# A two-layer encoder in fp32r matmuls: input-norm rows spread by matmuls with ones, output projection with its contraction outside, and adding transfers for one weight set a layer

## The chip, the cores and the metric

The kernel runs on one core of one Trainium2 chip. The metric is the device time of one execution in microseconds (us), as a median over several runs. All times below are us unless marked ns. The engines are PE (TensorE; PEld is its weight load), DVE (VectorE), ACT (ScalarE), POOL (GpSimd) and SP (SyncE, which here only issues transfers).

## The reference

512 tokens of width 1024 pass an input LayerNorm and two layers. A layer has three token mixers, a gated merge of their outputs, an output projection and a SwiGLU feed-forward network (FFN), with a LayerNorm behind each residual sum:

```python
x = layer_norm(x, ln_in_g, ln_in_b)
for l in range(2):
    proj = x @ w_in[l]
    na, df, ml = neighbourhood(...), differential(...), latent(...)
    merged = sum(sigmoid(gate[b]) * (branch[b] @ w_branch[l, b]) for b in range(3))
    x = layer_norm(alpha * x + merged @ w_out[l], ln1_g[l], ln1_b[l])
    g, u = split(x @ w_ffn_in[l])              # 1024 -> 2 x 2816
    x = layer_norm(alpha * x + (silu(g) * u) @ w_ffn_out[l], ln2_g[l], ln2_b[l])
```

## The kernel before

Tokens are held as four tiles of 128 rows (`xt[t]`, width 1024) and, transposed and split, as `xth` and `xtl`. Every fp32 matmul is made of three fp32r products of a high and a low part (`mm3`, L155 to L158). Weights come in chunks of 512 KB by SP's queue into `raw` (two buffers); `wsplit` (L134) makes the high part on ACT (`whi`, L138) and the low part on DVE (`wlo`, L139), as a rule at high priority. A DVE or ACT operation of width 512 that is not a weight's split is mostly L221 and L222, the two halves of `split`.

Two families of slots hold the rest: `R` (38 of width 512) and `H` (8 of width 1024, named f0 to f7), both first in, first out. PSUM has four tags with two banks each: `acc`, `sc`, `pv` and `tr`. A scheduler sets the order on each engine when the program is built; code under `tc.high_priority()` is placed ahead of other work that is ready.

The places that matter here:

- **The start** (L280 to L294). SP loads the first token tile, the constants, the LayerNorm's scale and shift (`load_gb`, L266 to L271: one 4 KB row each, broadcast by the transfer to 128 partitions, 512 KB each), the second tile and two weight chunks. For each tile `layer_norm` (L234) takes statistics (L237, L239), a power on POOL, then the two passes L252 and L253 on DVE; for columns from `SPREAD` on, the passes go to ACT and POOL instead (L247 to L249). `to_xt` (L258) transposes a tile on PE in two groups of four (L263) and splits them (L221, L222).
- **The output projection** (`out_proj`, L701). For each half of 512 output columns it loads four weight chunks, and then, token tile by token tile, runs all eight contraction steps into one `acc` bank and adds the bank to the residual (L711). Between the halves `ahead()` takes the loads of the plain FFN weights (`plain_weights`; issued at L206, split by L221 and L222). The second half yields each tile to the LayerNorm and the transposes.
- **The FFN.** The first set of 256 hidden columns is `ffn_plain`. The ten other sets of a layer run as `ffn_fast` (L813): seven products of quarter size (L778) in place of eight, on sums of weight quarters (L839 s = u0 + u1, L840 u0 = g0 - u0, L841 g0 = s - g0, L853 g1 = g1 - g0, each 1024 wide on DVE) and on sums of `x` quarters, made once a layer by `x_sums` (L732, the adds at L748 to L759). The first fast set of a layer, `early`, loads its weights while the LayerNorm before it still runs; its first product is copied out by ACT (L833, `p1`), and the results are added at L844, L848 and later lines.

Of the kernel before, what the change touches and what calls it, by code (L numbers as in the profile page):

```python
# [20 lines left out]
D_FF = 2816  # L21
# [60 lines left out]
def trunk(ctx, tc, x, ln_in, w_in, feat, bias, lamv, w_mla, w_mlr, w_mlv, w_branch, w_out,  # L82
# [28 lines left out]
    ring = cp.tile([128, 256], F32, name="ring")  # L111
    at = [0]

# [166 lines left out]
    G.memset(expo, -0.5)  # L280
    load_x(0)
    nc.sync.dma_start(cons, cst)
    gb = load_gb(ln_in)
    na_v, na_slots = [], []
# [416 lines left out]
    def out_proj(xt, mg, l, ahead):  # L701
        act = tuple(KTiles(m) for m in mg)
        for hf in range(2):
            if hf == 1:
                ahead()
            c = slice(hf * 512, (hf + 1) * 512)
            ch = wload_ks(lambda a, e: [w_out[l, a:e, c]], 512, (2, 2, 2, 2))
            for t in range(NT):
                p = bank("acc")
                gemm_x(p, ch, slice(0, 512), act, tsl(t), KD)  # L710
                V.scalar_tensor_tensor(xt[t][:, c], xt[t][:, c], ALPHA, p, op0=OP.mult, op1=OP.add)  # L711
                if hf == 1:
                    yield t
        R.put(*mg[0], *mg[1])
# [17 lines left out]
    def x_sums():  # L732
# [5 lines left out]
        for i in range(2):  # L738
            ts = gate_tiles() + [dp.tile([128, 512], F32, tag="o32", name="xs", bufs=1)]
            t1, t2, d = (two(t) for t in ts)  # L740
            q = lambda a: a[:, 2 * i:2 * i + 2]

            def halves(n, t):
                hl = (R.get(), R.get())
                split(*hl, t)
                res[n].append(hl)

            V.tensor_sub(t1, q(h(0, 1)), q(h(0, 0)))  # L748
            V.tensor_sub(d, q(lo(0, 1)), q(lo(0, 0)))
            V.tensor_add(t1, t1, d)  # L750
            V.tensor_sub(t2, q(h(1, 1)), t1)
            V.tensor_add(t2, t2, q(lo(1, 1)))
            halves(1, ts[1])
            halves(0, ts[0])
            V.tensor_sub(d, t2, q(h(0, 0)))
            V.tensor_sub(d, d, q(lo(0, 0)))
            halves(2, ts[2])
            V.tensor_sub(t1, q(h(1, 0)), t2)
            V.tensor_add(t1, t1, q(lo(1, 0)))  # L759
            halves(3, ts[0])  # L760
# [19 lines left out]

    def hidden(gate, up):

        sg = ptile()
        A.activation(sg, gate, AF.Silu)
        V.tensor_mul(sg, sg, up)
        hl = (R.get(), R.get())
# [26 lines left out]
    def ffn_fast(l, m, sums):  # L813
# [3 lines left out]

        def load(t, base, kh):
            c = slice(base + m * 128, base + (m + 2) * 128)
            nc.sync.dma_start(t.rearrange("p (k c) -> p k c", k=4),  # L820
                              w_ffn_in[l, kh * 512:(kh + 1) * 512, c].rearrange("(k p) c -> p k c", p=128))
            return t
# [3 lines left out]

        g0, u0, u1 = load(H.get(), 0, 0), load(H.get(), D_FF, 0), load(H.get(), D_FF, 1)
        s = H.get()
        g1 = load(wp.tile([128, 1024], F32, tag="raw", name="raw", bufs=2), 0, 1)
        px, py, pz = bank("sc"), bank("pv"), bank("sc")  # L830
# [7 lines left out]
        with tc.high_priority():  # L838
            V.tensor_add(s, u0, u1)  # L839
            V.tensor_sub(u0, g0, u0)  # L840
            V.tensor_sub(g0, s, g0)  # L841
        product(py, halved(g0), from_sum(t2), True)
# [9 lines left out]
        with tc.high_priority():  # L852
            V.tensor_sub(g1, g1, g0)  # L853
        product(pz, halved(g1), from_x(1, 1), False)
        V.tensor_add(u2, pz, u2)
        product(py, halved(u1), from_sum(t4), False)
        V.tensor_add(p1, py, p1)
        H.put(s, u0, g0, u1)
        res = [hidden(px, p1)]
        res.append(hidden(u2, u3))  # L860
        return res
# [228 lines left out]
```

## Time and profile before

| what | value |
|---|---|
| median of 3 runs | 1858.38 us (1858.06 to 1862.17) |
| profiled execution | 1861.61 us, span 1859.6 us |
| PE busy | 1814.6 us, 98% of the span |
| DVE, ACT, POOL busy | 1331.0 (72%), 905.3 (49%), 88.2 (5%) us |
| transfers | 34.5% of 16 engines over the span, 105 GB/s |
| granted TensorE clock, mean | 0.996 |

A share of busy time is a mean over stages. The profiled execution is 3.2 us above the median of the runs shown; 2.0 of its 1861.61 us lie outside the span. A row of a timeline gives start, duration and, in brackets, how long the engine stood idle before and which work ended that wait. A row's duration is longer than its share of a queue when instructions overlap: what an instruction adds to its engine's queue is the distance to the next start.

### The profile page before, as it was taken

How to read it: one execution, taken by the hardware profiler on the slowest of the kernel's cores; microseconds unless marked ns; L12 is line 12 of the kernel's file. 1: busy time of each engine (PE TensorE's matmuls, PEld its weight loads, DVE VectorE, ACT ScalarE, POOL GpSimd, SP SyncE). 2: the span in 40 equal slices, each digit the busy share in tenths (PEclk: the TensorE clock that was granted, in tenths of full speed). 3: DMA queues.
4: the chain of work that ended last, by engine and by line, in shares of the span. 5: the costliest groups of instructions: out<-in, count | busy, mean ns of one | idle time of the engine just before them, and what ended most of it. 6: DMA issues, size and time to landing. Idle time of an engine off the chain costs nothing.

```text
span 1859.6 us, 28547 instructions
## 1 busy us (share of the span) xinstructions
PE 1814.6 (98%) x11200; PEld 1617.4 (87%) x11200; DVE 1331.0 (72%) x2228; ACT 905.3 (49%) x1620; POOL 88.2 (5%) x165
## 2 busy tenths in 40 slices
PE   6999999999999899999999999999999999999997
PEld 5988899988878899999789888999888789999996
DVE  6478887665568977777756888866655698677766
ACT  3467776555433433434326677755554244343431
POOL 4100000000001000000001000000000000000001
PEclk9999999999999999999999999999999999999999
DMA  7453332223251233333445432322233512333332
GB/s 250 119 166 88 88 101 74 79 81 85 90 193 58 69 104 101 102 103 102 148 124 156 124 97 87 90 65 86 74 97 109 174 57 90 105 95 110 92 101 79
DMA packets 167765, 195.86 MB, mean 105 GB/s; under 512 B 8528, under 2 KB 132688, under 8 KB 167632
## 3 DMA queue, kind: packets, MB, share of 16 engines
q1 hardware_dynamic: 167632, 194.05, 34.5%
q8 instruction: 88, 1.44, 0.3%
q14 instruction: 45, 0.37, 0.1%
HBM read 177.24 MB, written 9.44 MB: 100 GB/s over the span
## 4 chain that ended last, share of the span: by engine, by line
PE 89%; DVE 4%; DMA 3%; ACT 2%; issue 1%; POOL 1%; POOLq 0%; SPq 0%; DVEq 0%; ACTq 0%
PE acc L156 18%; PE acc L157 18%; PE acc L158 18%; PE sc L778 11%; PE pv L778 8%; PE tr L648 2%; DVE wlo L139 1%; PE pv L491 1%; DMA raw<-in_w_ffn_in_dram 1%; ACT whi L138 1%; PE pv L656 1%; PE pv L655 1%; PE sc L477 1%; PE sc L632 1%; PE sc L631 1%
## 5 line engine op out<-in xcount | busy, mean ns | idle before, releaser
L139 DVE TENSOR_TENSOR wlo<-raw,whi 128x1024 fp32r<-128x1024 f32 (+4 forms) x242 | 288.0, 1191 | 137.0 <-ACT whi L138 132.2
L138 ACT ACTIVATE whi<-raw 128x1024 fp32r<-128x1024 f32 (+4 forms) x242 | 250.0, 1034 | 267.4 <-DMA raw<-in_w_ffn_out_dram 50.9
L138 ACT ACTIVATE whi<-f 128x1024 fp32r<-128x1024 f32 x100 | 104.9, 1057 | 222.4 <-PE acc L158 127.3
L156 PE MATMUL acc<-xth,whi 128*128 128x512 f32 x512 | 203.9, 398 | 0.1
L158 PE MATMUL acc<-xth,wlo 128*128 128x512 f32 x512 | 202.8, 396 | 0.0
L157 PE MATMUL acc<-xtl,whi 128*128 128x512 f32 x512 | 202.6, 396 | 0.0
L156 PE MATMUL acc<-whi,r 128*128 128x512 f32 (+1 forms) x504 | 194.7, 392 | 4.6 <-DVE f L711 3.9
L157 PE MATMUL acc<-wlo,r 128*128 128x512 f32 (+1 forms) x504 | 197.3, 391 | 1.1 <-DVE wlo L139 1.1
L158 PE MATMUL acc<-whi,r 128*128 128x512 f32 (+1 forms) x504 | 197.0, 391 | 0.0
L778 PE MATMUL pv<-r,whi 128*128 128x256 f32 x960 | 175.8, 282 | 9.9 <-DVE P L844 4.8
L156 PE MATMUL acc<-whi,xth 128*128 128x256 f32 (+2 forms) x544 | 161.6, 299 | 2.1 <-ACT whi L138 2.1
L157 PE MATMUL acc<-wlo,xth 128*128 128x256 f32 (+2 forms) x544 | 162.1, 299 | 1.3 <-DVE wlo L139 1.3
L158 PE MATMUL acc<-whi,xtl 128*128 128x256 f32 (+2 forms) x544 | 162.1, 299 | 0.0
L778 PEld LDWEIGHTS pv<-r,whi 128*128 128x128 f32 x960 | 148.2, 189 | 13.4 <-DVE P L844 5.2
L139 DVE TENSOR_TENSOR wlo<-f,whi 128x1024 fp32r<-128x1024 f32 x100 | 121.6, 1221 | 26.0 <-ACT whi L138 25.8
L778 PE MATMUL pv<-r,wlo 128*128 128x256 f32 x480 | 134.7, 281 | 0.0
L778 PE MATMUL sc<-xth,whi 128*128 128x256 f32 x480 | 133.9, 280 | 0.7 <-ACT P L833 0.7
L778 PE MATMUL sc<-xtl,whi 128*128 128x256 f32 x480 | 133.7, 279 | 0.0
L778 PE MATMUL sc<-xth,wlo 128*128 128x256 f32 x480 | 133.3, 279 | 0.0
L156 PEld LDWEIGHTS acc<-whi,r 128*128 128x128 f32 x504 | 94.3, 188 | 26.9 <-DVE f L711 4.7
L157 PEld LDWEIGHTS acc<-wlo,r 128*128 128x128 f32 x504 | 95.0, 188 | 22.1 <-DVE wlo L139 1.8
L158 PEld LDWEIGHTS acc<-whi,r 128*128 128x128 f32 x504 | 94.9, 188 | 21.0
(235 smaller groups left out, 4285.3 us busy)
## 6 DMA issues: line engine op xcount, KB each, us to landing
raw<-in_w_in_dram SPq DMA_DIRECT2D x64, 512.0 KB, 3.8
f<-in_w_ffn_in_dram SPq DMA_DIRECT2D x60, 512.0 KB, 3.7
raw<-in_w_ffn_out_dram SPq DMA_DIRECT2D x44, 512.0 KB, 3.8
raw<-in_w_in_dram SPq DMA_DIRECT2D x64, 256.0 KB, 3.3
raw<-in_w_ffn_in_dram SPq DMA_DIRECT2D x28, 512.0 KB, 3.6
raw<-in_w_branch_dram SPq DMA_DIRECT2D x24, 512.0 KB, 3.5
raw<-in_w_out_dram SPq DMA_DIRECT2D x16, 512.0 KB, 3.8
r<-r SPq DMA_DIRECT2D x56, 128.0 KB, 2.9
```

The source lines that it names most:

```text
L138: A.activation(hi[:, :n], raw[:, :n], AF.Copy)
L139: V.tensor_sub(lo[:, :n], raw[:, :n], f32(hi[:, :n]))
L156: T.matmul(o, lh[0], rh[0], start=first, stop=False)
L157: T.matmul(o, lh[0], rh[1], start=False, stop=False)
L158: T.matmul(o, lh[1], rh[0], start=False, stop=last)
L477: T.matmul(sc, qs[j][:, tsl(t)], ks[j][1], start=False, stop=True)
L491: T.matmul(po[:, 0:256], ch_[:, tsl(k)], v, start=k == 0, stop=False)
L631: T.matmul(sc, q[0][:, tsl(t)], k[0], start=True, stop=False)
L632: T.matmul(sc, q[0][:, tsl(t)], k[1], start=False, stop=False)
L648: T.transpose(pt[:, tsl(i)], prs[i % 2][:, tsl(kp + i // 2)], ident)
L655: T.matmul(oc, v, ph[:, c], start=kt == 0, stop=False)
L778: T.matmul(o[:, c], w[a][:, j, f], x[e], start=fresh and mi == 0 and j == 0 and n == 0, stop=j == 3 and n == 2, skip_group_check=True)
```

## The change

1. **Start.** The first token tile comes in two halves, from SP's and ACT's queue. The LayerNorm's scale and shift come as two rows of 4 KB into one partition each; four matmuls with a row of ones (contraction 1) spread them over the partitions into `sc` and `pv` banks, and four ACT copies bring them to SBUF.
2. **Output projection.** In the first half the loop over weight chunks is outside and the four token tiles inside, each with a bank of its own (sc, sc, pv, pv), all added to the residual at the end. The second half keeps its loops, but its chunks are now asked for behind the plain FFN weights' place: `ahead()` has moved behind `wload_ks`.
3. **Early set.** For the first fast set of each layer, s is loaded as u0 and then u1 is added to it by a transfer that accumulates, issued by POOL; g0 is added to u0 in the same way. The two DVE adds of these fall away in this set. So that sums are enough, signs are flipped in the `x` sums, the weight sums and in `hidden` (by a form of instruction with a factor), for all sets. The slots are taken and returned in another order.

```diff
-    load_x(0)
+    nc.sync.dma_start(xt[0][:, 0:512], x[0:128, 0:512])
+    nc.scalar.dma_start(xt[0][:, 512:1024], x[0:128, 512:1024])
     nc.sync.dma_start(cons, cst)
-    gb = load_gb(ln_in)
+    rows = [H.get() for _ in range(2)]
+    for i in range(2):
+        nc.sync.dma_start(rows[i][0:1], ln_in[i:i + 1, :])
+    ones = ring[0:1, 0:128]
+    V.memset(ones, 1.0)
+    gb = []
+    for i, tag in enumerate(("sc", "pv")):
+        t = H.get()
+        for hf in range(2):
+            c = slice(hf * 512, (hf + 1) * 512)
+            p = bank(tag)
+            T.matmul(p, ones, rows[i][0:1, c], start=True, stop=True)
+            A.activation(t[:, c], p, AF.Copy)
+        gb.append(t)
+    H.put(*rows)
...
         for hf in range(2):
-            if hf == 1:
-                ahead()
             c = slice(hf * 512, (hf + 1) * 512)
             ch = wload_ks(lambda a, e: [w_out[l, a:e, c]], 512, (2, 2, 2, 2))
+            if hf == 0:
+                ps4 = [bank(i) for i in ("sc", "sc", "pv", "pv")]
+                for part in ch:
+                    for t in range(NT):
+                        gemm_x(ps4[t], [part], slice(0, 512), act, tsl(t), KD)
+                for t in range(NT):
+                    V.scalar_tensor_tensor(xt[t][:, c], xt[t][:, c], ALPHA, ps4[t], op0=OP.mult, op1=OP.add)
+                continue
+            ahead()
             for t in range(NT):
...
-            V.tensor_sub(t2, q(h(1, 1)), t1)
-            V.tensor_add(t2, t2, q(lo(1, 1)))
+            less(t2, q(h(1, 1)), t1)
+            V.tensor_sub(t2, t2, q(lo(1, 1)))
...
-        V.tensor_mul(sg, sg, up)
+        V.scalar_tensor_tensor(sg, up, sign, sg, op0=OP.mult, op1=OP.mult)
...
+            if add:
+                nc.gpsimd.dma_start(dst, src, accum_op=OP.add)
+            else:
+                nc.sync.dma_start(dst, src)
...
-        g0, u0, u1 = load(H.get(), 0, 0), load(H.get(), D_FF, 0), load(H.get(), D_FF, 1)
+        g0 = load(H.get(), 0, 0)
         s = H.get()
+        u0, u1 = load(H.get(), D_FF, 0), load(H.get(), D_FF, 1)
+        if early:
+            load(load(s, D_FF, 0), D_FF, 1, True)
+            load(u0, 0, 0, True)
...
         with tc.high_priority():
-            V.tensor_add(s, u0, u1)
-            V.tensor_sub(u0, g0, u0)
-            V.tensor_sub(g0, s, g0)
+            if not early:
+                V.tensor_add(s, u0, u1)
+                V.tensor_add(u0, g0, u0)
+            V.tensor_add(g0, s, g0)
...
         with tc.high_priority():
-            V.tensor_sub(g1, g1, g0)
+            V.tensor_add(g1, g1, g0)
...
-        H.put(s, u0, g0, u1)
+        H.put(g0, s, u0, u1)
```

Three places show what this does to the order of the engines. The rows name line, operation, output, inputs and shape.

DVE at the start, before (f0 and f1 are the first two token tiles, f4 and f5 the scale and the shift, tr a bank of transposes, wlo a low part of a weight chunk):

```order
L237 BN_STATS ring_126<-f0_112 128x6 x2
L239 BN_AGGR ring_126<-ring_126 128x2
L252 SCALAR_TENSOR_TENSOR f0_112<-f0_112,ring_126,f4_116 128x512
L252 SCALAR_TENSOR_TENSOR f0_112<-f0_112,ring_126,f4_116 128x256
L253 SCALAR_TENSOR_TENSOR f0_112<-f0_112,ring_126,f5_117 128x512
L253 SCALAR_TENSOR_TENSOR f0_112<-f0_112,ring_126,f5_117 128x256
L237 BN_STATS ring_126<-f1_113 128x6 x2
L222 TENSOR_TENSOR xtl_73<-tr_161,xth_72 128x4x128
```

The same place now (f6 and f7 are the scale and the shift):

```order
L252 SCALAR_TENSOR_TENSOR f0_112<-f0_112,ring_126,f6_118 128x512
L239 BN_AGGR ring_126<-ring_126 128x2
L252 SCALAR_TENSOR_TENSOR f1_113<-f1_113,ring_126,f6_118 128x512
L139 TENSOR_TENSOR wlo_150<-raw_147,whi_149 128x1024
L252 SCALAR_TENSOR_TENSOR f0_112<-f0_112,ring_126,f6_118 128x256
L139 TENSOR_TENSOR wlo_156<-raw_153,whi_155 128x1024
L237 BN_STATS ring_126<-f2_114 128x6 x2
L253 SCALAR_TENSOR_TENSOR f0_112<-f0_112,ring_126,f7_119 128x512
L253 SCALAR_TENSOR_TENSOR f1_113<-f1_113,ring_126,f7_119 128x512
L237 BN_STATS ring_126<-f3_115 128x6 x2
L253 SCALAR_TENSOR_TENSOR f0_112<-f0_112,ring_126,f7_119 128x256
```

The first tile's second pass (L253), which the first transposes wait for, stands behind both weight chunks' low parts and other tiles' work; its xtl split stands further down, behind the low part of a third chunk.

PE where the output projection begins in layer 0, before (acc_5365 and acc_5391 are the first half's first two token tiles, acc_5417 the third, r the merged inputs):

```order
L156 MATMUL acc_5365<-whi_5361,r24_98 128x512
L157 MATMUL acc_5365<-wlo_5362,r24_98 128x512
L158 MATMUL acc_5365<-whi_5361,r25_99 128x512
L157 MATMUL acc_5391<-wlo_5362,r26_100 128x512
L158 MATMUL acc_5391<-whi_5361,r27_101 128x512
L156 MATMUL acc_5391<-whi_5361,r24_98 128x512
L157 MATMUL acc_5391<-wlo_5362,r24_98 128x512
L158 MATMUL acc_5391<-whi_5361,r25_99 128x512
L156 MATMUL acc_5417<-whi_5343,r12_86 128x512
```

The same projection now (sc_5379 to pv_5382 are the four token tiles of the first half, acc_5235 and acc_5252 belong to the last merges):

```order
L158 MATMUL acc_5235<-r10_84,wlo_5232 128x512
L156 MATMUL sc_5379<-whi_5357,r12_86 128x512
L156 MATMUL sc_5380<-whi_5357,r12_86 128x512
L156 MATMUL pv_5381<-whi_5357,r12_86 128x512
L156 MATMUL pv_5382<-whi_5357,r12_86 128x512
L156 MATMUL acc_5252<-r34_108,whi_5231 128x512
L157 MATMUL acc_5252<-r35_109,whi_5231 128x512
```

The first half no longer needs the bank of a tile that DVE still has to add, and its matmuls now stand among those of the last merges.

DVE ahead of the transposes' splits in layer 0, before (f6 and f4 are the third and fourth token tile, tr_5552 and tr_5559 the transposes of the first tile, tr_5601 the first of the second, wlo_5928 and wlo_5958 the early set's g0 and g1):

```order
L711 SCALAR_TENSOR_TENSOR f6_118<-f6_118,acc_5615 128x512
L253 SCALAR_TENSOR_TENSOR f5_117<-f5_117,ring_126,f2_114 128x512 x2
L237 BN_STATS ring_126<-f6_118 128x6
L139 TENSOR_TENSOR wlo_5928<-f1_113,whi_5927 128x1024
L239 BN_AGGR ring_126<-ring_126 128x2
L139 TENSOR_TENSOR wlo_5958<-raw_5922,whi_5957 128x1024
L222 TENSOR_TENSOR xtl_73<-tr_5552,xth_72 128x4x128
L252 SCALAR_TENSOR_TENSOR f6_118<-f6_118,ring_126,f7_119 128x512 x2
L222 TENSOR_TENSOR xtl_73<-tr_5559,xth_72 128x4x128
L711 SCALAR_TENSOR_TENSOR f4_116<-f4_116,acc_5664 128x512
L253 SCALAR_TENSOR_TENSOR f6_118<-f6_118,ring_126,f2_114 128x512
L222 TENSOR_TENSOR xtl_73<-tr_5601,xth_72 128x4x128
```

The same place now (f1 is g0 and f0 is s of the early set; tr_5566 and tr_5573 are the first tile's transposes, tr_5615 the first of the second, L733 is the second half's add to the residual):

```order
L139 TENSOR_TENSOR wlo_5975<-raw_5939,whi_5974 128x1024
L874 TENSOR_TENSOR f1_113<-f0_112,f1_113 128x1024
L222 TENSOR_TENSOR xtl_73<-tr_5566,xth_72 128x4x128
L222 TENSOR_TENSOR xtl_73<-tr_5573,xth_72 128x4x128
L239 BN_AGGR ring_126<-ring_126 128x2
L733 SCALAR_TENSOR_TENSOR f6_118<-f6_118,acc_5678 128x512
L886 TENSOR_TENSOR raw_5939<-raw_5939,f1_113 128x1024
L139 TENSOR_TENSOR wlo_6044<-f1_113,whi_6043 128x1024
L252 SCALAR_TENSOR_TENSOR f4_116<-f4_116,ring_126,f5_117 128x512 x2
L237 BN_STATS ring_126<-f6_118 128x6
L139 TENSOR_TENSOR wlo_6074<-f0_112,whi_6073 128x1024
L222 TENSOR_TENSOR xtl_73<-tr_5615,xth_72 128x4x128
```

Two weight sums (L874, L886) and two more low parts, all four 1024 wide, now stand ahead of the second tile's splits; before, the early set's sums stood behind them. Of the plain FFN weights' eight low parts (L222 from raw), the last two now stand behind the second half's first add (L733), among the LayerNorm passes of the first tile; before, all eight stood ahead of that add (L711).

## Rows read from the trace of the kernel before

**Rows 1.** First part of the page: busy time by engine.
```profile
PE 1814.6 (98%) x11200; PEld 1617.4 (87%) x11200; DVE 1331.0 (72%) x2228; ACT 905.3 (49%) x1620; POOL 88.2 (5%) x165
```

**Rows 2.** Waits of PE: who released it, sum, times, longest.
```profile
PE pv L778 <- DVE P L844: 4.8, 2, 2.4
PE acc L156 <- DVE f L711: 3.9, 2, 2.2
PE pv L778 <- DVE r L222: 2.6, 2, 1.3
PE pv L778 <- DVE P L848: 2.3, 4, 1.0
PE tr L263 <- DVE xtl L222: 2.1, 2, 1.1
```

**Rows 3.** Timeline of PE in the output projection's first half, layer 0.
```profile
541.52 0.50 PE L156 MATMUL acc<-whi,r 128*128 128x512 f32 x1 [2.25 <-DVE f L711]
```

**Rows 4.** Windows: span, busy by engine, then PEclk (granted clock), DMA share, GB/s.
```profile
541.00:545.20 4.20, 3.68 (x10) 2.86 (x11) 3.45 (x6) 1.15 (x2) 0.00 (x0) 0.62 0.38 126
1537.20:1541.00 3.80, 3.76 (x23) 3.76 (x24) 3.48 (x3) 0.00 (x0) 0.00 (x0) 0.69 0.00 0
```

**Rows 5.** Timeline of PE in the early fast set, layer 0, then layer 1.
```profile
616.62 0.39 PE L778 MATMUL pv<-r,whi 128*128 128x256 f32 x1 [1.32 <-DVE r L222]
621.29 0.50 PE L778 MATMUL pv<-r,whi 128*128 128x256 f32 x2 [2.40 <-DVE P L844]
625.42 0.51 PE L778 MATMUL pv<-r,whi 128*128 128x256 f32 x2 [1.04 <-DVE P L848]
1542.37 0.51 PE L778 MATMUL pv<-r,whi 128*128 128x256 f32 x2 [0.78 <-DVE P L848]
```

**Rows 6.** Timeline of DVE from the second half's first add to the early set, layer 0.
```profile
564.59 0.69 DVE L711 SCALAR_TENSOR_TENSOR f<-f,acc 128x512 f32<-128x512 f32 x1 [3.48 <-PE acc L158]
...
575.26 1.23 DVE L139 TENSOR_TENSOR wlo<-raw,whi 128x1024 fp32r<-128x1024 f32 x1
576.40 0.68 DVE L222 TENSOR_TENSOR xtl<-tr,xth 128x512 fp32r<-128x512 f32 x1
577.00 1.40 DVE L252 SCALAR_TENSOR_TENSOR f<-f,ring,f 128x512 f32<-128x512 f32 x2
578.32 0.68 DVE L222 TENSOR_TENSOR xtl<-tr,xth 128x512 fp32r<-128x512 f32 x1
...
580.18 0.68 DVE L222 TENSOR_TENSOR xtl<-tr,xth 128x512 fp32r<-128x512 f32 x1
...
583.30 1.40 DVE L252 SCALAR_TENSOR_TENSOR f<-f,ring,f 128x512 f32<-128x512 f32 x2
...
589.20 1.23 DVE L839 TENSOR_TENSOR f<-f,f 128x1024 f32<-128x1024 f32 x1 [2.56 <-DMA f<-in_w_ffn_in_dram]
```

**Rows 7.** Timeline of PE at the plain FFN's start, layer 0.
```profile
578.92 0.39 PE L156 MATMUL sc<-xth,r 128*128 128x256 f32 x1 [0.69 <-ACT xth L221]
...
580.92 0.66 PE L263 MATMUL tr<-cons,f 128*128 128x128 f32 x4 [1.05 <-DVE xtl L222]
```

**Rows 8.** Timeline of ACT: the early set's first product copied out, layer 0.
```profile
609.34 0.58 ACT L833 ACTIVATE P<-sc 128x512 f32<-128x512 f32 x1
```

**Rows 9.** Timeline of DVE, PE and PE at the start.
```profile
8.45 1.61 DVE L252 SCALAR_TENSOR_TENSOR f<-f,ring,f 128x512 f32<-128x512 f32 x2 [2.63 <-DMA f<-in_ln_in_dram]
...
11.25 1.97 PE L263 MATMUL tr<-cons,f 128*128 128x128 f32 x8 [11.25 <-DVE f L253]
...
17.02 0.63 PE L158 MATMUL acc<-whi,xtl 128*128 128x512 f32 x1
```

**Rows 10.** Transfers: line, count, KB each, median from issue to landing.
```profile
f<-in_w_ffn_in_dram SPq DMA_DIRECT2D x60, 512.0 KB, 3.7
...
f<-in_x_dram SPq DMA_DIRECT2D x4, 512.0 KB, 9.4
```

**Rows 11.** Forms of L225, two tensors and a factor: min, median, max in ns.
```profile
L225 DVE SCALAR_TENSOR_TENSOR r<-f,r x16: 681/688/693, 511.3 to 1451.0; 128x512 fp32r<-128x512 f32 x16
```

More of the change, by code (lines that the diff above doesn't have):

```diff
@@ L111, in trunk @@
     ring = cp.tile([128, 256], F32, name="ring")
-    at = [0]
+    at = [128]
     def stat(w=1):
@@ L711, in out_proj @@
                 V.scalar_tensor_tensor(xt[t][:, c], xt[t][:, c], ALPHA, p, op0=OP.mult, op1=OP.add)
-                if hf == 1:
-                    yield t
+                yield t
         R.put(*mg[0], *mg[1])
@@ L746, in halves, with less @@
                 res[n].append(hl)
-            V.tensor_sub(t1, q(h(0, 1)), q(h(0, 0)))
-            V.tensor_sub(d, q(lo(0, 1)), q(lo(0, 0)))
+            def less(o, a, b):
+                V.scalar_tensor_tensor(o, a, -1.0, b, op0=OP.mult, op1=OP.subtract)
+            V.tensor_sub(t1, q(h(0, 0)), q(h(0, 1)))
+            V.tensor_sub(d, q(lo(0, 0)), q(lo(0, 1)))
             V.tensor_add(t1, t1, d)
-            V.tensor_sub(t2, q(h(1, 1)), t1)
-            V.tensor_add(t2, t2, q(lo(1, 1)))
+            less(t2, q(h(1, 1)), t1)
+            V.tensor_sub(t2, t2, q(lo(1, 1)))
             halves(1, ts[1])
             halves(0, ts[0])
-            V.tensor_sub(d, t2, q(h(0, 0)))
+            less(d, t2, q(h(0, 0)))
             V.tensor_sub(d, d, q(lo(0, 0)))
             halves(2, ts[2])
-            V.tensor_sub(t1, q(h(1, 0)), t2)
-            V.tensor_add(t1, t1, q(lo(1, 0)))
+            less(t1, q(h(1, 0)), t2)
+            V.tensor_sub(t1, t1, q(lo(1, 0)))
             halves(3, ts[0])
@@ L779, in product, with hidden @@
                              stop=j == 3 and n == 2, skip_group_check=True)
-    def hidden(gate, up):
+    def hidden(gate, up, sign=1.0):
         sg = ptile()
         A.activation(sg, gate, AF.Silu)
-        V.tensor_mul(sg, sg, up)
+        V.scalar_tensor_tensor(sg, up, sign, sg, op0=OP.mult, op1=OP.mult)
         hl = (R.get(), R.get())
@@ L816, in ffn_fast, with load @@
         early = not sums
-        def load(t, base, kh):
+        def load(t, base, kh, add=False):
             c = slice(base + m * 128, base + (m + 2) * 128)
-            nc.sync.dma_start(t.rearrange("p (k c) -> p k c", k=4),
-                              w_ffn_in[l, kh * 512:(kh + 1) * 512, c].rearrange("(k p) c -> p k c", p=128))
+            src = w_ffn_in[l, kh * 512:(kh + 1) * 512, c].rearrange("(k p) c -> p k c", p=128)
+            dst = t.rearrange("p (k c) -> p k c", k=4)
+            if add:
+                nc.gpsimd.dma_start(dst, src, accum_op=OP.add)
+            else:
+                nc.sync.dma_start(dst, src)
             return t
@@ L857, in ffn_fast @@
         V.tensor_add(p1, py, p1)
-        H.put(s, u0, g0, u1)
-        res = [hidden(px, p1)]
-        res.append(hidden(u2, u3))
+        H.put(g0, s, u0, u1)
+        res = [hidden(px, p1, -1.0)]
+        res.append(hidden(u2, u3, -1.0))
         return res
```

## The prediction
> **What bounds the kernel now.** I read the page's first part first: PE is busy for 1814.6 of 1859.6 us [rows 1]. No matmul of the layers is removed, so the change can win only what PE loses between matmuls, and each part must be judged by which wait of PE it ends and which one it makes. So the second view was PE's waits: the largest inside the layers come from DVE [rows 2]. Third came the timelines around each of them, and last the windows, for the granted clock after a wait.
>
> Three places lose time in a layer. In the output projection's first half, PE waits 2.25 us in layer 0 for a bank that L711 has to empty [rows 3]; both layers together lose 3.9 [rows 2], so layer 1 loses 1.6. At the plain FFN's start PE waits 0.69 and 1.05 for the split transposes [rows 7]. In the early fast set it waits 1.32, 2.40 and 1.04 in layer 0 [rows 5]; in layer 1 the first two are the same, by the totals and their longest [rows 2], and the third is 0.78 [rows 5]. After two of these waits the granted clock falls: 0.62 of full speed in the 4.20 us behind the projection's wait, 0.69 in 3.80 us of layer 1's early set [rows 4]. A mean between 0.5 and 1 means that a part ran at 1.2 and the rest at 2.4 GHz. The cost is the busy time by the missing share: 3.68 x 0.38 = 1.4 and 3.76 x 0.31 = 1.2 us.
>
> **Output projection: what goes.** With four banks for four tiles the bank wait ends: 2.25 in layer 0, with its slow stretch 1.4, so 3.7; 1.6 in layer 1. The new order also lets the first half's matmuls stand among the last merges, so that PE has other work while weights come. The second half's first bank may now wait for DVE, where plain weights' splits stand: one such split is 0.6 us of DVE's queue (from 576.40 to 577.00 [rows 6]), and I charge that one, 0.6 a layer, bounds 0 and 2.2 (the wait it had).
>
> **Early set: what goes.** L839 and L840, of one form, each hold DVE for 1.23 us [rows 6]; without them, and with g0, g1 and two low parts done long before, the `x` sums come earlier than PE needs them. I take all three waits as gone: 1.32 + 2.40 + 1.04 = 4.8 in layer 0; 1.32 + 2.40 + 0.78 = 4.5 in layer 1, with the slow stretch 1.2, so 5.7. PE also loses about 0.16 us of refill at each wait (the row behind the 2.40 wait lasts 0.50 where 0.39 is usual [rows 5]; an estimate): four waits, 0.6 in each layer. Removed in all: 3.7 + 4.8 + 0.6 = 9.1 in layer 0, 1.6 + 5.7 + 0.6 = 7.9 in layer 1. The form with a factor costs what a plain add does, 0.688 against 0.68 [rows 11, 6], so the flipped signs cost nothing.
>
> **Plain FFN's start: what comes.** This is the term that decides. The transposes of the second token tile can be used only when DVE has split them. Before, from the second half's first add (564.59) to that split (580.18) DVE works through 15.6 us almost without a gap [rows 6], and PE still has to wait. The order now puts two weight sums and two low parts between the same two points, at 1.14 each (from 575.26 to 576.40 [rows 6]): 4.6. Two plain splits and a statistics pass are added and one LayerNorm pass (1.40 for two overlapped, 0.66 in the queue: 577.00 to 578.32 [rows 6]) falls behind: 3 x 0.6 - 0.66 = 1.1. The last plain weight chunk is also issued later, behind the projection's second half. A transfer of 512 KB takes 3.7 from issue to landing [rows 10]; DVE stands between 0 and 2.2 us before it (3.7 less the 1.5 us of work ahead of it), and I take 0.8. The wait of PE there grows by 4.6 + 1.1 + 0.8 = 6.5. Its upper end is 4.6 + 1.1 + 2.2 = 7.9; its lower end is 3, if DVE's 3.48 us of idling just ahead of the first add [rows 6] could take 2.7 of the 5.7. PE would stand there for about 8 us instead of 1.7, and after 2.25 us the clock already fell [rows 3, 4]; so I add a slow stretch of 1.4. Added: 0.6 + 6.5 + 1.4 = 8.5 a layer. So layer 0 wins 0.6 and layer 1 loses 0.6: the wait of the early set has moved ahead, to the transposes, at nearly its old size.
>
> **Adding transfers.** The trace shows none issued by POOL. Their bounds are the median of a plain 512 KB weight load, 3.7, and that of the crowded start, 9.4 [rows 10]; I take 4, since the queues are as empty here as for the 3.7. The one for u0 is the later: its slot held the LayerNorm's scale until the last L252 pass, which ends near 584.7 [rows 6] and now, with DVE 6.5 later, near 591; its plain load lands by 595. ACT splits u0 just ahead of copying the first product out, which it did at 609.34 [rows 8] and will do near 614, PE being 0.6 + 6.5 + 1.4 - 3.7 = 4.8 later there. That leaves 19 us: cover for both 4 and 9.4, so the cost is nothing. For s there are more, since its base needs no LayerNorm slot. On POOL the transfer for s stands ahead of the LayerNorm's powers and waits for its base, loaded during the projection's first half, long before a power is due; the one for u0 stands behind the powers, so nothing in the LayerNorm waits for it. On SP the set asks for one 512 KB load more (the base of s); with POOL's two that is three more transfers a layer, some 4 us each in a stretch where no wait of PE names a transfer [rows 2]: nothing.
>
> The Trainium skill speaks against this part. Its page SBUF — State Buffer, section SBUF: two separate sides, holds that a transfer issued from POOL can be left without descriptors while DVE runs an operation that takes a port both share; the section after it gives 620 ns alone and 3100 ns beside one. Five times the 3.7 of a row would be 18.5 us, an estimate by that page, just inside the 19. The same page, section Who interferes with whom, leaves adds of two tensors out of the operations that do this, and the rows of DVE here are such adds and passes with a factor; no row here shows such a transfer.
>
> **Start.** Two transfers of 512 KB fall away, for whose data the first L252 waited 2.63 us, to 8.45 [rows 9]. The four matmuls with ones and their ACT copies come instead. A plain fp32 matmul of 512 columns is in no row; between 0.39 (a quick fp32r one, [rows 5]) and four passes at the slow 0.63 [rows 9], 2.5 us each, all lie in the time that PE idles anyway, up to 11.25 [rows 9]; I take 0.63, and the scale is there near 7 us instead of 8.4. But the first transposes wait for L253, and the order now puts ahead of it four statistics passes of the second and third tile, a first pass for the second tile and two chunks' low parts: 4 x 0.6 + 0.7 + 2 x 1.14 = 5.4 us of DVE by the durations in [rows 6]. So transposes start near 14 instead of 11.25, and PE's steady work, at 17.02 before [rows 9], near 19.5, held by the first tile's split behind a third low part. The last four transposes of a later tile then lie ahead of it, which gives some of it back. I take 1.5 lost, bounds -1 (the scale's earlier arrival carries through) and 4 (2.8 from the transposes and another low part).
>
> **Sum.** 1.5 - 0.6 + 0.6 = +1.5 on the profiled 1861.61, 1863.1. That execution is 3.2 above the median of the runs shown; so 1859.9 as a median, within the 0.3% (5.6 us) that a measurement of this kernel can tell from no change.
>
> **Rivals.**
> - *The extra DVE work finds cover* (faster). If the weight sums and low parts fall where the split would have waited for ACT or PE anyway, PE's wait grows by 3 and its clock holds. For it: the page has DVE at 72%, and the first bank's add at 564.59 comes after 3.48 us of idling [rows 6], time that earlier adds could free. Against it: behind 564.59 the rows have no gap. A layer then adds 0.6 + 3 = 3.6 against 9.1 and 7.9: -5.5 - 4.3 + 1.5 = -8.3, 1850.
> - *The last plain chunk comes late* (slower). DVE's two splits of it stand in its queue ahead of the LayerNorm's passes, so that everything behind waits. Where that load lands 3.8 us after DVE is ready for it instead of 0.8 (a whole 3.7 us transfer, issued only when the buffer is free), each layer loses 3 more: 1859.9 + 6 = 1866. It decides from some 2.8 us on. For it: only two buffers, both in use by the projection's chunks. Against it: ACT and DVE have PE's whole second half to empty them.
> - *u0's adding transfer outlasts its cover* (slower). From 19 us after its issue on, ACT's split of u0 blocks the copy behind it, on which two adds and PE's next product hang. At 30 us it costs 11 a layer: 1882. The rows' nearest transfers, 3.7 and 9.4 [rows 10], speak against it. The Trainium skill's page named above would bring it about.
> - *The wait merely moves* is the forecast itself.
>
> **How the numbers follow.** The forecast has 0.53 (0.46 within 0.3%, 0.05 below, 0.02 above), cover found 0.25, the late chunk 0.15, the outlasting transfer 0.07. So faster by over 0.3% is 0.05 + 0.25 = 0.30, within it 0.46, slower 0.02 + 0.15 + 0.07 = 0.24. The range 1849 to 1867 holds the first three cases but for their ends (start at -1 or 4, the growth at 3 or 7.9) and leaves out the transfer: about 0.8. The forecast's own range is 1854 to 1865.
>
> **What would show it.** Right: no wait of PE for the first half's add; none in the early set for L222 or the additions that were L844 and L848; a wait of PE at the second tile's transposes of 6 to 9 us with a slow stretch behind it; first transposes near 14 us; the add transfers landed before 605. Wrong: a wait there under 4 us, waits on L139 of the early set's u0, or a start at or under 17 us to steady work.

## The result

The change is slower: 1878.08 us (1875.18 to 1879.11, 5 runs) against 1860.03 (1858.06 to 1864.31, 5 runs), a ratio of 1.0091 with a 95% interval of 1.0074 to 1.0109. The prediction said 1859.9 with a range of 1849 to 1867; it was wrong. The profiled executions differ by 16.5 us (1878.08 against 1861.61), so the traces hold what has to be explained.

### The profile after

First part of the page of the changed kernel, as in [rows 1]:

```profile
PE 1827.6 (97%) x11208; PEld 1625.5 (87%) x11208; DVE 1329.5 (71%) x2225; ACT 905.8 (48%) x1624; POOL 95.0 (5%) x169
```

Waits of PE, as in [rows 2] (sum, times, longest):

```profile
PE sc L157 <- DVE xtl L222: 9.2, 2, 4.7
PE tr L263 <- DVE xtl L222: 6.0, 3, 2.5
PE sc L802 <- ACT P L865: 5.5, 2, 2.9
PE sc L295 <- DVE ring L237: 5.2, 1, 5.2
PE tr L263 <- DVE f L253: 3.1, 1, 3.1
PE acc L157 <- DVE wlo L139: 2.3, 2, 1.6
PE sc L156 <- ACT xth L221: 1.4, 2, 0.7
PE acc L156 <- DVE f L733: 1.4, 2, 0.8
```

The first half's add (3.9 before) is gone, and so are the early set's waits for L844, L222 and L848 of [rows 2]. In their place stand 9.2 and 6.0 for the split transposes, and, new, 5.5 for L865, the copy of a fast set's first product. The timeline of PE shows where (the start, the plain FFN of layer 0, the third fast set):

```profile
15.44 1.12 PE L263 MATMUL tr<-cons,f 128*128 128x128 f32 x4 [3.05 <-DVE f L253]
...
22.31 0.78 PE L158 MATMUL acc<-whi,xtl 128*128 128x512 f32 x1
...
581.27 1.25 PE L263 MATMUL tr<-cons,f 128*128 128x128 f32 x8 [2.46 <-DVE xtl L222]
583.25 0.53 PE L156 MATMUL sc<-xth,r 128*128 128x256 f32 x1 [0.73 <-ACT xth L221]
...
588.46 0.58 PE L157 MATMUL sc<-xtl,r 128*128 128x256 f32 x1 [4.46 <-DVE xtl L222]
...
669.00 0.58 PE L802 MATMUL sc<-xth,whi 128*128 128x256 f32 x1 [2.89 <-ACT P L865]
```

Windows behind two of these waits (granted clock in the third place from the end, as in [rows 4]):

```profile
588.00:594.00 6.00, 5.54 (x28) 5.55 (x29) 5.26 (x9) 0.00 (x0) 1.70 (x2) 0.54 0.13 35
669.00:672.00 3.00, 3.00 (x14) 3.00 (x15) 2.11 (x3) 0.46 (x1) 0.00 (x0) 0.50 0.67 211
```

The granted clock of 0.54 and 0.50 means that nearly all of both stretches ran at 1.2 GHz.

### Where the time went

To add up small waits and slow stretches, I counted for each matmul how far its start lies behind the sum of the usual distances of all matmuls ahead of it (0.233 us for 512 columns, 0.118 for 256, 0.109 for a transpose, 0.154 for 336, as PE runs them without waits at the full clock). What this lag grows by in a stage is what PE lost there. Stages: the start (the first 70 us of PE's work), and in each layer the output projection with the last merges, the plain FFN, the early set, and the second to fourth fast set. The runs e1 to e13 are told below; the last column is the median of their runs, the kernel before being between 1860.0 and 1861.9 in all comparisons. The lags are those of one profiled execution each, whose time lies up to 2.5 us from the median, and kernels with the same start differ by up to 2.7 in that column; a difference of a microsecond in one cell says little.

| run | start | proj. 0 | plain 0 | early 0 | sets 2-4, 0 | proj. 1 | plain 1 | early 1 | sets 2-4, 1 | us |
|---|---|---|---|---|---|---|---|---|---|---|
| before | 19.3 | 4.0 | 2.4 | 6.0 | 0.0 | 1.7 | 2.4 | 7.3 | 0.0 | 1860.0 |
| after | 23.1 | 0.9 | 11.2 | 0.6 | 6.5 | 1.1 | 9.8 | -0.1 | 8.4 | 1878.1 |
| e1 put order | 22.8 | 2.0 | 10.7 | -0.1 | 2.5 | 3.8 | 9.7 | -0.1 | 3.5 | 1872.3 |
| e2 before, put order | 18.3 | 1.9 | 2.4 | 5.7 | 0.0 | 1.7 | 3.9 | 5.0 | 4.2 | 1862.8 |
| e3 old start | 17.5 | 3.8 | 10.0 | 0.6 | 8.0 | 0.7 | 9.6 | -0.1 | 8.8 | 1879.5 |
| e4 late s | 22.6 | 1.0 | 5.8 | 5.2 | -0.1 | 4.0 | 4.3 | 5.3 | 0.2 | 1866.2 |
| e5 copy first | 22.8 | 0.8 | 10.9 | 0.4 | 4.5 | 1.8 | 9.6 | -0.1 | 4.8 | 1873.3 |
| e6 start alone | 24.4 | 3.9 | 2.4 | 2.5 | 0.3 | 4.0 | 2.4 | 6.8 | -0.1 | 1863.2 |
| e7 projection alone | 17.8 | 0.9 | 4.9 | 1.6 | 0.3 | 0.8 | 3.4 | 2.1 | 0.3 | 1852.1 |
| e8 combined | 18.7 | 2.6 | 6.1 | 3.0 | 2.5 | 0.6 | 6.1 | 4.4 | 0.9 | 1864.8 |
| e9 put order, copy first | 21.7 | 1.5 | 10.4 | -0.4 | 2.3 | 3.7 | 9.8 | -0.1 | 2.3 | 1871.2 |
| e10 early set alone | 18.6 | 1.7 | 6.5 | 0.8 | 6.4 | 3.6 | 5.4 | 0.3 | 5.7 | 1867.7 |
| e11 start, projection | 22.7 | 0.7 | 5.6 | 4.0 | 4.0 | 1.9 | 5.0 | 1.8 | 4.6 | 1869.1 |
| e12 projection, POOL | 19.0 | 0.8 | 5.1 | 2.3 | -0.1 | 0.8 | 4.7 | 4.4 | 0.3 | 1856.5 |
| e13 e11, copy first | 23.2 | 0.8 | 5.7 | 4.0 | 1.2 | 1.6 | 4.9 | 5.6 | -0.6 | 1866.1 |

Before and after: start +3.8; projection -3.1 and -0.6; plain FFN +8.8 and +7.4; early set -5.4 and -7.4; sets 2 to 4 +6.5 and +8.4. The rest (attention, later sets, last LayerNorm) makes the remainder of -1.6. The waits the change was aimed at did move ahead to the transposes, at nearly the same size in all. The stages behind them, on which the prediction has no term, hold 14.9 of the 16.8 us that the lag grew by.

In the third fast set the chain reads as follows. DVE, from the late load of u1 (L872 is the sum s = u0 + u1, L886 that of g1):

```profile
654.45 1.23 DVE L872 TENSOR_TENSOR f<-f,f 128x1024 f32<-128x1024 f32 x1 [1.33 <-DMA f<-in_w_ffn_in_dram]
...
665.13 1.22 DVE L886 TENSOR_TENSOR raw<-raw,f 128x1024 f32<-128x1024 f32 x1
```

ACT, which splits that g1 and another weight before it copies the first product out (in the first row it has waited for DVE):

```profile
665.24 0.63 ACT L221 ACTIVATE r<-P 128x512 fp32r<-128x512 f32 x1 [3.05 <-DVE P L809]
...
666.46 1.06 ACT L138 ACTIVATE whi<-raw 128x1024 fp32r<-128x1024 f32 x1
667.42 1.04 ACT L138 ACTIVATE whi<-f 128x1024 fp32r<-128x1024 f32 x1
668.37 0.58 ACT L865 ACTIVATE P<-sc 128x512 f32<-128x512 f32 x1
```

The product that the copy reads was complete by 654.9: PE's matmuls into that bank ran from 651.06 and were followed by others at 654.54. ACT stood idle for 3.05 us before 665.24. So the copy was ready long before and had idle time to run in; it stood behind two splits, the first of which waited for DVE. ACT's order as built for this set, before and now (P is the copy's output, whi_6572 and whi_6587 the second split of g1):

```
L833 ACTIVATE P_6449<-sc_6418 128x512
L221 ACTIVATE r0_74<-P_6408 128x512
L138 ACTIVATE whi_6572<-raw_6416 128x1024

L138 ACTIVATE whi_6587<-raw_6431 128x1024
L138 ACTIVATE whi_6616<-f2_114 128x1024
L865 ACTIVATE P_6464<-sc_6433 128x512
```

No line of the diff touches this place. The two suspects were the slots (u1 now takes the slot that the set ahead reads last) and this order on ACT.

### The profile page after: what moved, and what is told of

The parts are those of the page before. It is cut to its first block, busy times and chain, and to the rows that moved or that the text cites. A ratio compares the mean times of both kernels' runs of the same rounds, so it can differ in the third digit from the quotient of the medians.

```text
span 1876.2 us, 28600 instructions
## 1 busy us (share of the span) xinstructions
PE 1827.6 (97%) x11208; PEld 1625.5 (87%) x11208; DVE 1329.5 (71%) x2225; ACT 905.8 (48%) x1624; POOL 95.0 (5%) x169
## 4 chain that ended last, share of the span: by engine, by line
PE 88%; DVE 6%; DMA 4%; ACT 1%; issue 1%; SPq 0%; POOLq 0%; DVEq 0%; POOL 0%; ACTq 0%
PE acc L157 17%; PE acc L158 17%; PE acc L156 17%; PE sc L802 10%; PE pv L802 7%; DVE wlo L139 2%; PE tr L663 2%; DMA f<-in_w_ffn_in_dram 1%; PE pv L506 1%; PE sc L157 1%; PE sc L158 1%; PE sc L156 1%; PE pv L157 1%; PE pv L158 1%; PE pv L156 1%
## 5 line engine op out<-in xcount | busy, mean ns | idle before, releaser
L139 DVE TENSOR_TENSOR wlo<-raw,whi 128x1024 fp32r<-128x1024 f32 (+4 forms) x242 | 287.8, 1190 | 135.0 <-ACT whi L138 133.7
L157 PE MATMUL acc<-wlo,r 128*128 128x512 f32 (+1 forms) x440 | 171.3, 389 | 2.3 <-DVE wlo L139 2.3
L156 PE MATMUL acc<-whi,r 128*128 128x512 f32 (+1 forms) x440 | 168.9, 391 | 2.7 <-DVE f L733 1.4
L158 PE MATMUL acc<-whi,r 128*128 128x512 f32 (+1 forms) x440 | 171.1, 389 | 0.0
L139 DVE TENSOR_TENSOR wlo<-f,whi 128x1024 fp32r<-128x1024 f32 x100 | 121.1, 1220 | 33.2 <-ACT whi L138 33.2
L156 PEld LDWEIGHTS acc<-xth,whi 128*128 128x128 f32 x512 | 96.3, 188 | 19.2 <-ACT f L687 0.5
L157 PEld LDWEIGHTS acc<-xtl,whi 128*128 128x128 f32 x512 | 96.4, 188 | 18.8
L158 PEld LDWEIGHTS acc<-xth,wlo 128*128 128x128 f32 x512 | 96.4, 188 | 18.7
```

The lines of the kernel that those rows point to most:

```text
L139: V.tensor_sub(lo[:, :n], raw[:, :n], f32(hi[:, :n]))
L156: T.matmul(o, lh[0], rh[0], start=first, stop=False)
L157: T.matmul(o, lh[0], rh[1], start=False, stop=False)
L158: T.matmul(o, lh[1], rh[0], start=False, stop=last)
```

## The experiments

**e1, the slots returned in another order.**

```diff
-        H.put(g0, s, u0, u1)
+        H.put(s, u1, u0, g0)
```

> The change, with one line different: a fast set returns its slots in the order s, u1, u0, g0, so that the next set's u1 no longer takes the slot that is read last. Theory 1 (slots): the third fast set's u1 comes late because its slot is the previous set's u1, read by the last split; then PE's wait in that set (2.9 us on the copied product, some 5.5 us with the slow clock in layer 0, some 7 in layer 1) goes, and the time falls by 10 to 13 us, to about 1865 to 1868. Rival (the extra work on DVE, or POOL's transfers, set the whole chain back, whatever the slots): the wait stays and the time falls by under 3 us.

Measured: 1872.28, ratio to before 1.0063 (1.0047 to 1.0079), so about 6 us of the 18, half of what the theory asked. L872 of the third set no longer waits for a transfer. But the scheduler now put the copy of the second set behind g1's second split (in layer 1 that of the third set too), and the wait came there:

```profile
645.75 0.39 PE L802 MATMUL sc<-xth,whi 128*128 128x256 f32 x1 [2.29 <-ACT P L865]
```

The slots are one cause, not the only one.

**e2, the change's slot order in the kernel before.** Slots taken and returned as g0, s, u0, u1; nothing else.

> The kernel before, with the change's order of taking (g0, s, u0, u1) and returning (g0, s, u0, u1) slots and nothing else. Theory 1 (slots): a wait of PE in the third fast set appears here too and the time grows by 8 to 13 us, to about 1868 to 1873. Rival (adding transfers or DVE's load are needed for it): within 3 us of the kernel before.

Measured: 1862.76, ratio 1.0005 (0.9996 to 1.0015), not to be told from the kernel before. The theory of slots alone fell. In layer 0 the copy stayed ahead of g1's second split and sets 2 to 4 lost nothing; in layer 1 the build put the second set's copy behind it, and they lost 4.2. Layer 0's projection (2.1 less) and layer 1's early set (2.3 less) gave about that much back.

**e3, the old start in the changed kernel.** The diff's first hunk undone.

> The change with the start of the kernel before (broadcast transfers in place of matmuls with ones). Theory: the start alone costs 4 to 5 us (PE stands 4.6 us further back at 47 us), so the time falls by 4 to 5, to about 1873 to 1874. Rival (the lag of the start is made up later, in waits that end at the same moment): it falls by under 1.5.

Measured: 1879.47, ratio to before 1.0103 (1.0084 to 1.0121): no gain. PE was 5.6 us ahead after the start, and lost it in the projection (3.8 against 0.9), sets 2 to 4 and the last LayerNorm. There both kernels stand at the same place at the same time, the second with a longer wait ahead of it. The changed kernel:

```profile
914.02 0.50 PE L156 MATMUL acc<-whi,r 128*128 128x512 f32 x1 [1.18 <-DVE f L911]
926.87 0.50 PE L157 MATMUL acc<-wlo,r 128*128 128x512 f32 x1 [0.77 <-DVE wlo L139]
```

With the old start:

```profile
912.70 0.50 PE L156 MATMUL acc<-whi,r 128*128 128x512 f32 x1 [2.72 <-DVE f L896]
926.85 0.50 PE L157 MATMUL acc<-wlo,r 128*128 128x512 f32 x1 [0.76 <-DVE wlo L139]
```

**e4, s on the late slot.** Taken as g0, u0, s, u1, returned as s, u0, u1, g0.

```diff
-        g0 = load(H.get(), 0, 0)
-        s = H.get()
-        u0, u1 = load(H.get(), D_FF, 0), load(H.get(), D_FF, 1)
+        g0, u0 = load(H.get(), 0, 0), load(H.get(), D_FF, 0)
+        s = H.get()
+        u1 = load(H.get(), D_FF, 1)
```

> The change with slots taken as g0, u0, s, u1 (returned s, u0, u1, g0): in the early set s now has the slot that the LayerNorm frees late, u0 the early one, and the weight sums with their low parts stand behind the second token tile's transposes. Theory (the four wide DVE operations make PE's wait at the plain FFN): the wait there falls from 7.6 us to about 2 to 3 with no slow clock, the early set stays without waits, and the time falls by 10 to 13 for the slots and 6 to 8 a layer for this, 22 to 29 in all, to about 1849 to 1856. Rival (the waits of the early set come back, since s is late): the time is that of the put order alone, 1865 to 1868, with waits of 2 to 5 us a layer in the early set.

Measured: 1866.15, ratio 1.0028 (1.0018 to 1.0038); the time of the rival, and both mechanisms. With the two sums and two low parts behind the second tile's splits, the wait for xtl fell from 4.46 to 1.94, and the plain FFN's loss from 11.2 to 5.8 and 9.8 to 4.3: the four wide operations were the larger part of it, with 2.4 lost before and the rest left. The early set's loss came back, from 0.6 to 5.2, since DVE reaches the sums late. In this build all copies stand ahead, the slots follow the kernel before's pattern, and sets 2 to 4 lost nothing. Two of its waits:

```profile
PE pv L802 <- DVE P L877: 5.1, 2, 2.5
PE sc L157 <- DVE xtl L222: 3.8, 2, 1.9
```

**e5, the copy ahead by a dependence.** For the second and third set, g1's sum reads a column made of the copied product.

```diff
+                z = stat()
+                V.tensor_scalar(z, p1[:, 0:1], 0.0, 1.0, op0=OP.mult, op1=OP.add)
+                V.scalar_tensor_tensor(g1, g1, z, g0, op0=OP.mult, op1=OP.add)
```

> The change, with g1's sum of the second and third fast set made to read a column of the copied first product (times 0, plus 1, so its value is unchanged), so that ACT's copy of that product stands ahead of g1's second split, as in the kernel before. Theory 2 (ACT's queue order): the third fast set's wait comes from this copy standing behind two splits that wait for DVE; then the stretch of the second to fourth set goes from 6.5 and 8.4 us lost to under 1.5 each, though the slots are unchanged, and the time falls by 11 to 14, to about 1864 to 1867. Rival (theory 1, slots and their late load alone): the wait only moves to another product of the same set and the time falls by under 4.

Measured: 1873.33, ratio 1.0069 (1.0052 to 1.0085), 4.8 us faster than the change. The wait for the copy is gone; the late u1 stayed and its chain now stops PE at smaller waits in other products:

```profile
650.51 0.48 PE L802 MATMUL pv<-r,whi 128*128 128x256 f32 x2 [0.87 <-DVE P L881]
660.30 0.50 PE L802 MATMUL pv<-r,whi 128*128 128x256 f32 x2 [1.07 <-DVE r L222]
661.25 0.50 PE L802 MATMUL sc<-r,whi 128*128 128x256 f32 x2 [0.44 <-ACT whi L138]
```

Between the two theories: of 6.5 and 8.4, this edit leaves 4.5 and 4.8, that of e1 2.5 and 3.5.

**e6, the start alone.** The first hunk in the kernel before.

> The kernel before with the change's start alone. Theory (the start's lag of 3.8 us is lost for good): about 1864 to 1866. Rival (a lag there is made up in later waits, as the old start in the changed kernel gained nothing): within 2 us of the kernel before.

Measured: 1863.16, ratio 1.0012 (1.0001 to 1.0022). PE is 5.1 us behind after the start, and the layer-0 early set loses 3.5 less. At 2.1 us above the kernel before, it lies at the edge of the rival's 2 us: about 3 of the 5.1 are made up, as e3 showed from the other side.

**e7, the projection alone.** The second hunk in the kernel before.

> The kernel before with the change's output projection alone. Theory of the prediction: the first half's wait and its slow clock go (4.0 and 1.7 us lost there in the two layers), the plain FFN's start is 1 to 2 us later a layer, so 1 to 3 us faster in all. Rival (the wait moves to the second half's first bank, 2 us as three of the changed builds show, with a slow clock): 0 to 3 us slower.

Measured: 1852.07, ratio 0.9953 (0.9939 to 0.9968). This version beats both kernels, by 9 us against before and by more than the theory asked. The projection loses 0.9 and 0.8 instead of 4.0 and 1.7, as predicted; the plain FFN loses 2.5 and 1.0 more and the early set 4.4 and 5.2 less. Its waits of PE inside the layers:

```profile
PE sc L157 <- DVE xtl L222: 3.9, 2, 1.9
PE pv L784 <- DVE P L850: 3.1, 2, 1.6
...
PE acc L156 <- DVE f L718: 1.2, 2, 0.6
```

In layer 0, DVE starts on the second half's first add at 560.08 instead of 564.59 [rows 6], and needs 55.0 us from there to the first add of the early set's results, where before it was 56.0 (L844 at 620.56). In layer 1 it needs 54.1 for 56.2. The stretch takes DVE nearly as long and starts sooner, so PE's waits end sooner:

```profile
560.08 0.68 DVE L718 SCALAR_TENSOR_TENSOR f<-f,acc 128x512 f32<-128x512 f32 x1
...
615.12 0.69 DVE L850 TENSOR_TENSOR P<-pv,P 128x512 f32<-128x512 f32 x1
```

The copy of the second set stands behind g1's second split here too, in both layers, and costs nothing: PE has no wait in sets 2 to 4. In layer 0 DVE's sum of g1 begins at 630.41, the copy ends at 633.29, and PE, still busy with other products, needs it at 633.34. In the change that sum begins at 665.13, when PE has 1.0 us of work left ahead of its wait. The order costs PE time where DVE comes late to g1, and here DVE is early:

```profile
630.41 1.22 DVE L859 TENSOR_TENSOR raw<-raw,f 128x1024 f32<-128x1024 f32 x1
```

**e8, the pieces combined.** e4 with the old start, the dependence of e5, and the first difference of the low parts in the `x` sums (two operations a layer) on POOL.

> The change with the late slot for s, the old start, the ordered copy of run e5, and the first difference of the low parts in the x sums on POOL instead of DVE (two operations a layer). Theory (DVE's work between the second half's first add and the early set's products is what all these waits share, so taking work off DVE is the only part that gains): the early set's loss falls from 5.2 to about 2 to 3 a layer and the time from 1866 to about 1857 to 1861. Rival (POOL's operation is slow enough, near 1.8 us as its 512-wide products at the start, to hold up the chain of x sums): 1863 to 1867, with PE waiting for L222 of an x sum.

Measured: 1864.76, ratio 1.0022 (1.0013 to 1.0031); the rival's range, though not by its mechanism alone: PE's waits for L222 in the fast sets add up to 1.0. The early set lost 3.0 and 4.4, less than e4's 5.2 and 5.3, but the plain FFN (12.2 in the two layers together, against 10.1) and sets 2 to 4 (3.4 against 0.1) lost more.

**e9, both edits of e1 and e5.**

> The change with both edits of runs e1 and e5: slots returned as s, u1, u0, g0, and g1's sum behind the copy in the second and third fast set. Theory (two causes, each about half: the late load of u1, and ACT's copy behind g1's second split): the loss in the second to fourth set falls from 6.5 and 8.4 us to under 1 in each layer, where either edit alone left 2.5 to 4.8, and the time is about 1863 to 1868. Rival (one cause that either edit only shifts): 3 to 5 us a layer stay there, time 1870 to 1873.

Measured: 1871.2, ratio 1.0056 (1.004 to 1.0071); 2.3 lost in sets 2 to 4 of each layer. That is less than either edit alone left (2.5 and 3.5; 4.5 and 4.8), and not the theory's "under 1". What remains there are waits of 0.6 and less on L139 and on the copy (L865) itself, though it stands ahead and no sum waits for u1; what makes them stays open. With 10 us lost at the plain FFN and 3.7 in layer 1's projection, it is only about 1 us faster than e1.

**e10, the early set alone.** The third part of the change in the kernel before.

> The kernel before with the change's early set alone (adding transfers, flipped signs, its order of slots). Theory (this part makes the whole loss: with the start alone at +2 and the projection alone at -9, the three parts add up only if it costs about 24): 1878 to 1890. Rival (the loss needs the projection's new order, which moves the plain weights behind it, together with the early sums): 1862 to 1872.

Measured: 1867.74, ratio 1.0042 (1.0027 to 1.0057). The parts do not add up: +2 (start), -9 (projection) and +6 make -1, and the change costs 18. Here the plain FFN loses 6.5 and 5.4, not 11.2 and 9.8; the projection's new order, which moves the plain weights behind it, is needed for the rest. The third set's copy stands behind g1's second split in both layers, and sets 2 to 4 lose 6.4 and 5.7.

**e11, start and projection, without the early set.**

> The change without its early set: start and projection changed, ffn_fast and x_sums as before. Theory: -9 and +2 add up, 1852 to 1856, with 5 to 8 us lost a layer from the projection to the early set. Rival (the start's lag shifts the scheduler's order in the projection and takes the gain away): 1858 to 1864.

Measured: 1869.06, ratio 1.0046 (1.0031 to 1.0061): 17 us slower than the projection alone, though the start alone costs 2, and above both expected ranges. Beside e7, it loses 4.9 more at the start, which no later stage makes up, and 8.0 more in sets 2 to 4. Slots and weight sums are those of the kernel before. The scheduler put the third set's copy behind g1's second split in layer 0 and the second set's in layer 1:

```profile
663.11 0.39 PE L799 MATMUL sc<-xth,whi 128*128 128x256 f32 x1 [2.29 <-ACT P L854]
```

**e12, the projection and one difference on POOL.** e7 with the two operations of e8 moved.

> The projection alone (run e7) with the first difference of the low parts in the x sums moved from DVE to POOL. Theory (DVE's work sets the early set): 1.2 us of DVE less in each layer, so 1 to 3 us faster than e7, 1849 to 1852. Rival (POOL's operation, near 1.8 us, holds up the x sums, or DVE's queue simply waits for it): the same as e7 or up to 3 slower.

Measured: 1856.5, ratio 0.9968 (0.9953 to 0.9984), some 3 us slower than e7 by the ratios and 4 by the medians: the rival. The early set loses 2.3 and 4.4 instead of 1.6 and 2.1. DVE's queue waits for POOL, for 2.4 us where four operations of some 0.6 were taken off it, so nothing was won:

```profile
DVE gt L756 <- POOL xs L755: 2.4, 2, 1.2
```

**e13, e11 with the ordered copy.** The edit of e5 in e11. The orders of SP and POOL are the same in both. PE's, against what was expected, is not: by the two traces 656 of its 11208 rows stand at another place, though the products just ahead of layer 0's wait are the same.

> Start and projection of the change (run e11), with the ordered copy of run e5 and nothing else; the orders of PE, SP and POOL are those of e11. Theory (ACT's queue order: e11 lost 4.0 and 4.6 us in the second to fourth set because the scheduler put the copy of the third set's first product behind g1's second split, as in the full change, and not because of slots, which are those of the kernel before): the loss there falls to under 1 a layer and the time by 6 to 9, to 1860 to 1863. Rival (it only moves, as half of it did in run e5): 1865 to 1868, with 2 us or more a layer left there.

Measured: 1866.09, ratio 1.0026 (1.0017 to 1.0036), 3 us faster than e11. PE's waits for the copy fall from 5.0 to this row, and sets 2 to 4 from 4.0 and 4.6 to 1.2 and -0.6:

```profile
PE sc L799 <- ACT P L854: 0.4, 2, 0.2
```

So, with the slots of the kernel before, the order on ACT carries 2.8 of the 4.0 in layer 0. In layer 1, 3.8 of the 5.2 came back just ahead, in the early set (5.6 in place of 1.8), where PE's order had moved with the edit; the time fell by 3 us where 6 to 9 were expected.

## Why the prediction was wrong

**What bounds the kernel** was read rightly: PE's waits and the slow clock behind them hold the whole difference.

**Output projection: what goes.** Right: "3.7" and "1.6", less 0.6 added each, make 3.1 and 1.0; measured were 3.1 and 0.6. e7 shows that this part alone wins 9 us, of which these are less than half. The wait that I charged at the second half's first bank was 0.55 in layer 0.

**Early set: what goes.** Right in place and size: with the refills 5.4 and 6.3 were predicted for the two layers, 5.4 and 7.4 measured; no wait for L222 or for the additions is left there. The refill of 0.16 a wait was too large by its own row (0.50 less 0.39 is 0.11), by some 0.2 a layer.

**Plain FFN's start: what comes.** Right: in layer 0 PE waits 2.46 + 0.73 + 4.46 = 7.65 us there instead of 1.74, 5.9 more where 6.5 was said; the slow clock behind it cost 5.54 x 0.46 = 2.5 instead of 1.4. DVE shows the four operations where the order had them:

```profile
579.39 1.22 DVE L874 TENSOR_TENSOR f<-f,f 128x1024 f32<-128x1024 f32 x1
...
582.39 1.21 DVE L886 TENSOR_TENSOR raw<-raw,f 128x1024 f32<-128x1024 f32 x1
583.53 1.21 DVE L139 TENSOR_TENSOR wlo<-f,whi 128x1024 fp32r<-128x1024 f32 x1
...
586.59 1.21 DVE L139 TENSOR_TENSOR wlo<-f,whi 128x1024 fp32r<-128x1024 f32 x1
587.72 1.28 DVE L222 TENSOR_TENSOR xtl<-tr,xth 128x512 fp32r<-128x512 f32 x2
```

"Layer 0 wins 0.6 and layer 1 loses 0.6" came out as 0.3 lost and 0.6 won over these three stages.

**Start.** Too small, within its bounds: "I take 1.5 lost" was 3.8. Transposes began at 15.44 for "near 14", and steady work at 22.31 for "near 19.5". The working's own terms give about 15.2 for the transposes (11.25, less 1.4 for the earlier scale, plus 5.4 of DVE), not 14, and the matmuls with ones took some 1.8 us each where 0.63 was taken. But e3 shows that in this change the lag there is made up later, and e6 that most of it is in the kernel before, so this term did not make the result. In e11 it was not made up; what takes it up are later waits.

**Adding transfers.** No wait of PE names them. They took 6.6 at the median, between the bounds 3.7 and 9.4:

```profile
f<-in_w_ffn_in_dram POOLq DMA_DIRECT2D x4, 512.0 KB, 6.6
```

The 18.5 that was estimated from the Trainium skill's page SBUF — State Buffer, section SBUF: two separate sides, did not come: the four took 6.1 to 8.7. The section Who interferes with whom of the same page of the Trainium skill says that sums of two tensors were not seen to stall such a transfer, and this trace agrees as far as it goes: DVE was busy for 2.1 to 3.6 us of each, nearly all with such sums and passes with a factor. None of the copies that the first section speaks of ran beside one, so its case is not tested here; nor does a run show why they took more than the plain 3.7.

**The step that failed** is the sum itself: "1.5 - 0.6 + 0.6" ends with the early set, and has no term for the nine other fast sets of a layer. The cost there was taken as nothing without a place being looked up, although the diff changes how every set takes and returns slots and the built order on ACT had moved. Measured: 6.5 and 8.4 us in the second to fourth set. None of the rivals named it; the slower ones named other places.

The runs show two causes. One is the slot of u1: with the copy ahead in both, e9's slots cost 2.3 in each layer where e5's, the change's, cost 4.5 and 4.8. The traces agree: in the kernels with the change's slots and early set (after, e3, e5, e10), DVE's sum of u0 and u1 waits 0.9 to 2.7 us for a transfer in the second and third set of both layers, in e2, with the slots alone, in two of these four sets, and in no other kernel. The other cause is the copy of the first product behind g1's second split on ACT: with the same slots, e13 against e11 gave 2.8 and 5.2 (3.8 of the latter lost again one set earlier), and e5 against the change 2.0 and 3.6. These edits moved some of PE's matmuls too, so the sizes are not the copy's alone; that it makes a wait is seen in the chain above, where ACT had idle time for it.

Over all fifteen kernels, the layers in which a copy in the second or third set stands behind that split lost 2.5 to 8.8 in sets 2 to 4, e7's two excepted (0.3 each, DVE being early there); where it stands ahead, they lost 2.5 or less, e5's two excepted. The two costs don't simply add up: with the slots of e1, putting the copy ahead (e9) gave only 0.2 and 1.2. The order is a by-product: the projection, the start, the early set and the order of the slots each flip it in some combination, and no part of the diff asks for it.

Open stays why DVE's stretch in e7 is 1.0 and 2.1 us shorter, what the 2.3 left in e9 are, and why the last LayerNorm of e3 ends at the change's time.

## What to carry to other kernels

Where a scheduler orders the queues, a change has to be followed through all the stages that the build reordered, not only those that the diff names: compare the built order around each operation that PE waits for (here the copy of a product on ACT) in every repetition. A wait is worth removing only if the work behind it is not simply placed ahead of something that PE needs sooner; wide sums made early were paid for at the transposes. Measure the parts of a combined change apart: here one of three parts gained 9 us, and the three together lost 18.

## What the runs showed that was not expected

The matmuls with ones (contraction 1, plain fp32, 512 columns) leave two records each, and take 3.75 us for the first two, some 1.8 us each:

```profile
5.22 3.75 PE L295 MATMUL sc<-f,ring 1*128 1x512 f32 x4 [5.22 <-DVE ring L237]
```

Behind 7 us of them PE was not at its full pace: at 22.88 and 23.31 its matmuls of 512 columns still start 0.43 us apart, as from 17.02 on before [rows 9], where 0.233 is usual. PE had stood idle in between, for 3.05, 0.84 and 2.07 us, and the profile's granted clock reads 1.00 in both stretches; so no run shows what held it.
